# Row sums of modulation vectors begun inside the attention, two more blocks of them as row sums, and a denser pace at the long convolution

## The chip, the cores and the metric

The kernel runs on one core of one Trainium2 chip. The metric is the device time of one launch in microseconds (us). A core has a matrix engine (TensorE, PE in the rows), a vector engine (VectorE, DVE), an activation engine (ScalarE, ACT), a general engine (GpSimd, POOL) and a queue engine (SyncE, SP). They run side by side, each through its own list of instructions in a fixed order, and wait for one another by semaphores. [...]

## What is computed

A batch of one with 256 tokens of width 1024 goes through two blocks of two layers. Every layer has a mixer and a feed-forward part (FFN), and each of the two is fed by a normalised input that is scaled and shifted, and added back through a gate. The six vectors for that (two shifts, two scales, two gates, 1024 numbers each) come from a conditioning vector by one product for each layer. Of the four mixers the first is a state-space part beside an attention, the second a convolution with 31 taps, the third a latent attention, the fourth a long convolution. In short:

```python
mod = silu(c) @ mod_w[layer] + mod_b[layer]            # 1024 -> 6 * 1024, for each layer
sh1, sc1, g1, sh2, sc2, g2 = split(mod, 6)
h = rms_norm(x, norm_g) * (1 + sc1) + sh1
x = x + g1 * mixer(h)
h = rms_norm(x, norm_g) * (1 + sc2) + sh2
x = x + g2 * ffn(h)

def latent_attention(h):                               # third mixer, 16 heads
    q = rms_norm(h @ w_dq, g_q) @ w_uq                 # and a rotation of 32 of its 96 columns
    k, v = keys and values from h @ w_dkv and a context
    return softmax(q @ k.T / sqrt(96)) @ v @ w_o

def long_convolution(u):                               # fourth mixer
    x1, x2, v = split(dwconv3(u @ w_in + b_in), 3)
    v = v * x2
    return ((fftconv(v, filters) + v * d_bias) * x1) @ w_out + b_out
```

## The kernel before

**Weights.** All is float32, carried as a high and a low part. A weight comes from memory in pieces of 128 x 1024 (512 KB) on SP's queue (L434). ScalarE copies a piece into its high part `hi` (L418), VectorE makes the low part `lo` as the difference (L419), and TensorE does three products for each step of the inner dimension: high by high (L443), high by low (L445), low by high (L444). The buffers for `hi` and `lo` are three deep, so VectorE and ScalarE run at most three pieces ahead of TensorE. `linear` walks over the blocks of 128 outputs of a product, `linear_tok` does it with tokens as the rows.

**Modulation vectors.** The `mod` of a layer is 48 blocks of 128 numbers. There are two ways to get them. `modulation` gives the work to TensorE: a step loads two tiles of 512 KB on SP's queue and does two products with each (L543, `mo<-raw,cs`, 32 x 512, four records a tile); four such steps make two groups of 512 numbers, and one transposition and one sum at the end finish all. `dotted_with` gives it to VectorE as row sums, called dots here: GpSimd issues the load of one block's 128 rows (L515, `mraw<-modt`, three buffers), VectorE multiplies it by the conditioning row `crow` and sums along the row (L517, with a short read of the accumulator), and after the last block of a call adds the bias (L519).

**Their order.** `also` puts dots into a list, `later` puts steps of `modulation` into another, each with the number of the place that needs them. `tick` is called after each block of `linear` or `linear_tok` with the share of a full piece that it did: it counts, and lets one dot go for each `pace` that has been counted (and one step of `modulation` for each `every`). `need(n)` lets all go that are due by place n. `down` runs the last product of a part: it sets a pace of its own for the first blocks and 1000 for the rest. The first blocks of a product behind a normalisation (a `Front`) don't tick. A dot that the code places is then moved further by the scheduler that puts each engine's instructions in order; what it chose is fixed in the program.

**The attention.** `layer_mla` does 16 heads as eight pairs j. `scores` makes four tiles of 128 x 512 for a pair: TensorE makes `s`, VectorE its maximum (`smax`, L1533), ScalarE the exponential into `sp` with its sum (L1535), VectorE the reciprocal (`sinv`, L1536), GpSimd scales the tile by it (L1537). `turned` has TensorE transpose the four tiles (into `sx` and `ax`, L1549), ScalarE and VectorE copy them to `pt` (L1553 on VectorE), and `heads` multiplies by the values into `o` (L1565), whose low part VectorE splits off as `hl` (L419). Pairs j and j+1 overlap; the pieces of queries and keys of pair j+2 stand between, and they run out at j = 6. Behind the loop comes `w_o` by `down`. Its results go into x (L754), and the squares of x (L710, `n`) into the next norm's sum. Behind the fifth block the Front of the FFN needs the gain `a21` (L741) and makes its operands `zh` and `zl` (L304).

**Stages in time** (us from the span's start): first mixer to 187, its FFN to 333, convolution of 31 taps to about 500, its FFN with the context of the attention to about 740, latent attention to 868, `w_o` to 887, its FFN to 1078, long convolution to 1237 (its `hy_out` from 1211), last FFN to the end.

## Time and profile before

| what | before |
| --- | --- |
| time, median of 3 runs | 1439.99 us (1439.74 to 1444.86) |
| profiled execution | 1446.99 us, its span 1445.0 us |
| busy share of the span | TensorE 94%, VectorE 82%, ScalarE 58%, GpSimd 10% |
| mean granted clock of TensorE | 0.973 |
| dots | 120, of 1226 ns each |
| chain that ended last | TensorE 68%, issue 15%, VectorE 10%, ScalarE 3%, DMA 3% |

The chain that ended last is followed back from the last instruction, from each to what released it. The average says that TensorE is nearly always busy; a stage can differ from it, so the stages around the change are read one by one.

### The profile page before, as it was taken

The page shows a single profiled execution, that of the slowest core. Times are in us where ns is not written, and L with a number is a line of the kernel's source. Part 1 is how long each engine was busy: PE and PEld are TensorE (multiplying, and loading weights), DVE is VectorE, ACT ScalarE, POOL GpSimd, SP SyncE. Part 2 cuts the span into 40 slices and gives each one's busy share as a digit, 9 for nine tenths or more (in the row PEclk, how much of TensorE's full clock was granted, in tenths as well). Part 3 has the DMA queues.
Part 4 walks back from the last instruction along what each step waited for, and adds up shares of the span by engine and source line. Part 5 has one row for each costly group of instructions (what it writes and reads, how often), then busy time and mean ns, then how long its engine had stood idle before and what let it go on. Part 6 is the DMA issues. An engine that isn't in the chain of part 4 may idle for free.

```text
span 1445.0 us, 28181 instructions
## 1 busy us (share of the span) xinstructions
PE 1361.3 (94%) x10702; PEld 1238.6 (86%) x10702; DVE 1184.4 (82%) x2379; ACT 837.5 (58%) x1562; POOL 151.1 (10%) x204
## 2 busy tenths in 40 slices
PE   6988899999998899999989999999999899999997
PEld 3666799999995898999977779999999668999997
DVE  7967888878697697888769867999888978799954
ACT  5533676554474575665457645866556645776642
POOL 1053000101000000001004650000110000000000
PEclk9998999999998999999989999999999899999998
DMA  9567576888757558878635435577795556557660
GB/s 367 205 158 277 202 262 220 277 256 289 245 175 291 177 175 338 277 233 266 213 95 161 137 119 198 155 244 247 264 325 195 170 182 240 176 177 235 193 185 29
DMA packets 91988, 311.88 MB, mean 216 GB/s; under 512 B 10949, under 2 KB 13662, under 8 KB 91726
## 3 DMA queue, kind: packets, MB, share of 16 engines
q1 hardware_dynamic: 72830, 244.67, 50.7%
q0 software_dynamic: 17856, 64.36, 13.9%
q8 instruction: 84, 1.38, 0.4%
q10 hardware_dynamic: 1168, 1.06, 0.3%
q14 instruction: 50, 0.41, 0.1%
HBM read 308.73 MB, written 1.32 MB: 215 GB/s over the span
## 4 chain that ended last, share of the span: by engine, by line
PE 68%; issue 15%; DVE 10%; ACT 3%; DMA 3%; POOL 1%; DVEq 0%; SPq 0%; POOLq 0%; ACTq 0%
PE mm L443 18%; PE mm L445 18%; PE mm L444 18%; DVE lo L419 3%; PE mo L543 2%; ACT hi L418 1%; PE o L1565 1%; PE ax L1665 1%; DVE mraw L517 1%; DMA raw<-ab_in 1%; PE sx L638 1%; PE s L443 1%; PE s L444 1%; POOL mraw L515 1%; PE s L445 1%
## 5 line engine op out<-in xcount | busy, mean ns | idle before, releaser
L418 ACT ACTIVATE hi<-raw 128x1024 fp32r<-128x1024 f32 (+3 forms) x402 | 404.0, 1007 | 371.4 <-PE mm L444 285.4
L419 DVE TENSOR_TENSOR lo<-raw,hi 128x1024 fp32r<-128x1024 f32 (+3 forms) x402 | 464.1, 1161 | 121.3 <-ACT hi L418 119.5
L443 PE MATMUL mm<-hh,hi 128*128 128x256 f32 x1440 | 410.3, 288 | 14.0 <-ACT hi L418 6.4
L445 PE MATMUL mm<-hh,lo 128*128 128x256 f32 x1440 | 407.9, 285 | 5.7 <-DVE lo L419 5.7
L444 PE MATMUL mm<-hl,hi 128*128 128x256 f32 x1440 | 408.3, 285 | 1.6 <-DVE hl L1184 1.0
L443 PEld LDWEIGHTS mm<-hh,hi 128*128 128x128 f32 x1440 | 274.1, 192 | 34.7 <-issue 9.9
L445 PEld LDWEIGHTS mm<-hh,lo 128*128 128x128 f32 x1440 | 275.6, 192 | 8.4 <-DVE lo L419 6.7
L444 PEld LDWEIGHTS mm<-hl,hi 128*128 128x128 f32 x1440 | 275.5, 191 | 7.6 <-issue 3.6
L443 PE MATMUL mm<-ah,hi 128*128 128x256 f32 x704 | 199.1, 283 | 1.8 <-ACT hi L418 1.8
L445 PE MATMUL mm<-ah,lo 128*128 128x256 f32 x704 | 198.0, 282 | 2.2 <-DVE lo L419 2.0
L444 PE MATMUL mm<-al,hi 128*128 128x256 f32 x704 | 197.1, 281 | 0.0
L443 PE MATMUL mm<-zh,hi 128*128 128x258 f32 x608 | 173.7, 289 | 8.1 <-ACT zh L303 4.7
L515 POOL DMA_DIRECT2D mraw<-modt x120 | 64.1, 534 | 1096.1 <-DVE mraw L517 949.1
L445 PE MATMUL mm<-zh,lo 128*128 128x258 f32 x608 | 174.6, 288 | 0.9 <-DVE lo L419 0.7
L444 PE MATMUL mm<-zl,hi 128*128 128x258 f32 x608 | 174.0, 287 | 0.0
L517 DVE SCALAR_TENSOR_TENSOR mraw<-mraw,crow 128x1024 f32<-128x1024 f32 x120 | 145.9, 1226 | 5.7 <-DMA mraw<-modt 5.5
L445 PEld LDWEIGHTS mm<-ah,lo 128*128 128x128 f32 x704 | 132.5, 189 | 3.9 <-DVE lo L419 3.6
L443 PEld LDWEIGHTS mm<-ah,hi 128*128 128x128 f32 x704 | 132.8, 189 | 3.2 <-ACT hi L418 2.0
L444 PEld LDWEIGHTS mm<-al,hi 128*128 128x128 f32 x704 | 132.7, 189 | 1.0 <-issue 1.0
L443 PEld LDWEIGHTS mm<-zh,hi 128*128 128x128 f32 x608 | 117.1, 194 | 9.0 <-ACT zh L303 4.9
L445 PEld LDWEIGHTS mm<-zh,lo 128*128 128x128 f32 x608 | 117.2, 193 | 1.8 <-DVE lo L419 1.7
L444 PEld LDWEIGHTS mm<-zl,hi 128*128 128x128 f32 x608 | 117.9, 194 | 0.2 <-DVE zl L304 0.2
(427 smaller groups left out, 2119.8 us busy)
## 6 DMA issues: line engine op xcount, KB each, us to landing
raw<-up SPq DMA_DIRECT2D x132, 512.0 KB, 4.4
mraw<-modt POOLq DMA_DIRECT2D x120, 512.0 KB, 5.2
raw<-down SPq DMA_DIRECT2D x64, 512.0 KB, 4.4
raw<-mod SPq DMA_DIRECT2D x60, 512.0 KB, 5.2
raw<-gate SPq DMA_DIRECT2D x44, 512.0 KB, 4.7
raw<-down SPq DMA_DIRECT2D x32, 384.0 KB, 3.3
raw<-hy_in SPq DMA_DIRECT2D x24, 512.0 KB, 4.3
raw<-cm_in SPq DMA_DIRECT2D x16, 512.0 KB, 3.6
```

Source lines behind the costliest of these rows:

```text
L418: nc.scalar.activation(hi, src, AF.Copy)
L419: return nc.vector.tensor_tensor(lo, src, hi.bitcast(F32), op=ALU.subtract)
L443: nc.tensor.matmul(out, wh, xh, start=start, stop=False)
L444: nc.tensor.matmul(out, wh, xl, start=False, stop=False)
L445: self.last = nc.tensor.matmul(out, wl, xh, start=False, stop=stop)
L515: nc.gpsimd.dma_start(w, self.d[f"modt{layer}"][u])
L517: nc.vector.scalar_tensor_tensor(w, w, 1.0, row, op0=ALU.mult, op1=ALU.mult, accum_out=out[:, u : u + 1]))
L543: nc.tensor.matmul(acc[g * 32 : g * 32 + 32, :], wt, src, start=(g not in begun), stop=last)
L638: last = self.nc.tensor.matmul(st[:, c0 + t : c0 + t + 1], q[:, t * P : (t + 1) * P], self.ones[:, 0:1], start=(i == 0), stop=(i == len(sq ...
L1565: nc.tensor.matmul(o[i * 64 : i * 64 + 64], vals[:, k, c : c + 64], pt[i][:, k, :], start=(k == 0), stop=(k == 3))
L1665: nc.tensor.matmul(ps, m[:, k, m0 : m0 + P], src[:, k, s], start=(k == 0), stop=(k == 1))
```

## The change

Four things are altered. In the attention's loop over pairs a `tick` of 2.0 is added for the last three pairs, and the pace in `w_o` goes from 1.7 to 1.2. The dots of layer 2, blocks 40 to 48, and of layer 3, blocks 0 to 16, are put into the list ahead of the attention and no longer behind it. Blocks 16 to 24 of layer 3 are put there ahead of the FFN that follows and no longer at the long convolution; blocks 24 to 32, which were two of the four groups that `modulation` did at the long convolution, become dots beside them, and the steps of `modulation` that are left come at every fourth count and no longer at every second. In the convolution with 31 taps the pace goes from 2.0 to 1.5.

```diff
@@ -1584,9 +1584,11 @@
                 else:
                     qq = qq[1:] * 2
                 heads(j, pt)
+                if j > 4:
+                    self.tick(2.0)
             self.dump("mla_o", oh.bitcast(F32))
             self.need(6.5)
-            self.down(d["w_o"], oh, ol, self.residual(x, g1, sq, front=front), 1.7, acc=both)
+            self.down(d["w_o"], oh, ol, self.residual(x, g1, sq, front=front), 1.2, acc=both)
 
 
     def hy_filters(self, fp, hp, H):
@@ -1851,7 +1853,7 @@
 
         self.later(4, self.modulation(1, range(6, 9), cs, mods[1:2]), 1000.0)
         self.later(5, self.modulation(2, range(4), ("c_2", "c_ctx_2"), (mods[2], modc)), 2.0)
-        self.pace(2.0)
+        self.pace(1.5)
         self.also(4, 1, 36, 40, row, mods[1])
         f2.norm(self.stats(sq, D))
         sq = []
@@ -1907,6 +1909,8 @@
 
             e.close()
             sq = []
+            self.also(8, 2, 40, 48, row2[0], mods[2])
+            self.also(9, 3, 0, 16, row2[0], mods[3])
             f = front(7, 2, 3, "a21", "norm_ffn_g_2", 0)
             with self.banks(mm=2, s=2, ax=1, o=1):
                 self.layer_mla(x, f2, None, six(2, 2), sq, ckh, ckl, pe, final, f)
@@ -1914,8 +1918,8 @@
         self.dump("x4", x)
         e.enter_context(self.more(4))
         self.pace(3.0)
-        self.also(8, 2, 40, 48, row2[0], mods[2])
-        self.also(9, 3, 0, 16, row2[0], mods[3])
+        self.also(10, 3, 16, 24, row2[0], mods[3])
+        self.also(11, 3, 24, 32, row2[0], mods[3])
         f.norm(self.stats(sq, D))
         sq = []
         f2 = front(9, 3, 0, "a30", "norm_mix_g_2", 8)
@@ -1926,8 +1930,7 @@
             H = hyp.tile([P, 4, D], F32, name="H")
             f2.norm(self.stats(sq, D))
             self.pace(1.5)
-            self.later(11, self.modulation(3, range(6, 10), cs, mods[3:]), 2.0)
-            self.also(10, 3, 16, 24, row2[0], mods[3])
+            self.later(11, self.modulation(3, range(8, 10), cs, mods[3:]), 4.0)
             sq = []
             f = front(11, 3, 3, "a31", "norm_ffn_g_2", 8)
             self.layer_hy(x, f2, None, six(3, 2), sq, hyp, H, f)
```

The order of the instructions shows it as follows. Names with a number are tiles; `mraw` is a dot's tile.

At the end of the attention, VectorE before, from the first score tile of the last pair:

```order
L1533 TENSOR_REDUCE smax_10560<-s_10556 128x1
L1536 RECIPROCAL sinv_10443<-ssum_10442 128x1
L419 TENSOR_TENSOR hl_9343<-o_10519,hh_9342 128x256
L1533 TENSOR_REDUCE smax_10572<-s_10568 128x1
L1553 COPY pt4_10530<-ax_10537 128x4x128
L1536 RECIPROCAL sinv_10562<-ssum_10561 128x1
L1533 TENSOR_REDUCE smax_10584<-s_10580 128x1
L1536 RECIPROCAL sinv_10574<-ssum_10573 128x1
```

And in the changed kernel:

```order
L1533 TENSOR_REDUCE smax_10567<-s_10563 128x1
L1536 RECIPROCAL sinv_10569<-ssum_10568 128x1
L419 TENSOR_TENSOR hl_9343<-o_10519,hh_9342 128x256
L517 SCALAR_TENSOR_TENSOR mraw_10530,mod2_80<-mraw_10530,crow_7941 128x1024
L1533 TENSOR_REDUCE smax_10579<-s_10575 128x1
L1553 COPY pt4_10537<-ax_10544 128x4x128
L1533 TENSOR_REDUCE smax_10591<-s_10587 128x1
L519 TENSOR_TENSOR mod2_80<-mod2_80,p1_882 128x16
L517 SCALAR_TENSOR_TENSOR mraw_10534,mod2_80<-mraw_10534,crow_7941 128x1024
L1536 RECIPROCAL sinv_10581<-ssum_10580 128x1
```

Two dots now stand here. The reciprocal of the first tile (before `sinv_10562`, now `sinv_10569`) has moved ahead of both; a dot stands ahead of the maximum of the second tile (`smax_10579`), and another ahead of its reciprocal (before `sinv_10574`, now `sinv_10581`).

GpSimd at the same place before, from the last scaling of the pair before the last:

```order
L1537 TENSOR_SCALAR sp_10445<-sp_10445,sinv_10443 128x512
L1537 TENSOR_SCALAR sp_10564<-sp_10564,sinv_10562 128x512
L1537 TENSOR_SCALAR sp_10576<-sp_10576,sinv_10574 128x512
L1537 TENSOR_SCALAR sp_10588<-sp_10588,sinv_10586 128x512
L1537 TENSOR_SCALAR sp_10600<-sp_10600,sinv_10598 128x512
L515 DMA mraw_11878<-modt2 128x1024
```

And in the changed kernel:

```order
L1537 TENSOR_SCALAR sp_10445<-sp_10445,sinv_10443 128x512
L1537 TENSOR_SCALAR sp_10571<-sp_10571,sinv_10569 128x512
L515 DMA mraw_10662<-modt2 128x1024
L515 DMA mraw_10735<-modt2 128x1024
L1537 TENSOR_SCALAR sp_10583<-sp_10583,sinv_10581 128x512
L1537 TENSOR_SCALAR sp_10595<-sp_10595,sinv_10593 128x512
L1537 TENSOR_SCALAR sp_10607<-sp_10607,sinv_10605 128x512
L515 DMA mraw_10774<-modt2 128x1024
```

Two loads of dots now stand between the first and the second scaling of the last pair.

VectorE at the start of `w_o`, before, from the last low part of the attention's output:

```order
L419 TENSOR_TENSOR hl_9343<-o_10641,hh_9342 128x256
L754 SCALAR_TENSOR_TENSOR x_88<-s_10652,mod2_80,x_88 128x256
L754 SCALAR_TENSOR_TENSOR x_88<-mm_10686,mod2_80,x_88 128x256
L754 SCALAR_TENSOR_TENSOR x_88<-s_10726,mod2_80,x_88 128x256
L419 TENSOR_TENSOR lo_10766<-raw_10763,hi_10765 128x1024
L419 TENSOR_TENSOR lo_10802<-raw_10799,hi_10801 128x1024
L419 TENSOR_TENSOR lo_10838<-raw_10835,hi_10837 128x1024
L710 TENSOR_TENSOR n_10720<-n_10684,n_10718 128x256
L517 SCALAR_TENSOR_TENSOR mraw_10722,mod2_80<-mraw_10722,crow_7941 128x1024
```

And in the changed kernel:

```order
L419 TENSOR_TENSOR hl_9343<-o_10651,hh_9342 128x256
L517 SCALAR_TENSOR_TENSOR mraw_10662,mod2_80<-mraw_10662,crow_7941 128x1024
L754 SCALAR_TENSOR_TENSOR x_88<-s_10665,mod2_80,x_88 128x256
L754 SCALAR_TENSOR_TENSOR x_88<-mm_10699,mod2_80,x_88 128x256
L754 SCALAR_TENSOR_TENSOR x_88<-s_10738,mod2_80,x_88 128x256
L419 TENSOR_TENSOR lo_10781<-raw_10778,hi_10780 128x1024
L419 TENSOR_TENSOR lo_10820<-raw_10817,hi_10819 128x1024
L419 TENSOR_TENSOR lo_10859<-raw_10856,hi_10858 128x1024
L304 SCALAR_TENSOR_TENSOR zl_10894<-x_88,a21_10891,zh_10893 128x256
L710 TENSOR_TENSOR n_10733<-n_10697,n_10731 128x256
```

A dot has come between the last `hl` and the first result of `w_o`, and ahead of the three low parts that follow. Counted by the pieces of weights that stand ahead of them, the changed kernel has eight dots in the attention's last part and `w_o` where the one before had one: four between the last key piece and the first piece of `w_o` (one behind the last `hl`), and four in `w_o`. In the FFN behind, 24 dots become 23, at the same places.

VectorE in `hy_out` of the long convolution before, from a sum of squares ahead of the gain `a31`:

```order
L710 TENSOR_TENSOR n_15093<-n_15047,n_15091 128x256
L754 SCALAR_TENSOR_TENSOR x_88<-n_15126,mod3_81,x_88 128x256
L570 TENSOR_REDUCE mod3_81<-ax_15143 128x16
L571 TENSOR_TENSOR mod3_81<-mod3_81,p1_882 128x16
L741 SCALAR_TENSOR_TENSOR a31_15226<-mod3_81,p1_882 128x8
L419 TENSOR_TENSOR lo_15288<-raw_15285,hi_15287 128x1024
L710 TENSOR_TENSOR n_15131<-n_15093,n_15129 128x256
L419 TENSOR_TENSOR zl_15229<-mod3_81,zh_15228 128x8x2
L304 SCALAR_TENSOR_TENSOR zl_15229<-x_88,a31_15226,zh_15228 128x256 x2
```

And in the changed kernel:

```order
L517 SCALAR_TENSOR_TENSOR mraw_15043,mod3_81<-mraw_15043,crow_7941 128x1024
L754 SCALAR_TENSOR_TENSOR x_88<-n_15077,mod3_81,x_88 128x256
L570 TENSOR_REDUCE mod3_81<-ax_15136 128x8
L419 TENSOR_TENSOR lo_15281<-raw_15278,hi_15280 128x1024
L571 TENSOR_TENSOR mod3_81<-mod3_81,p1_882 128x8
L710 TENSOR_TENSOR n_15082<-n_15041,n_15080 128x256
L754 SCALAR_TENSOR_TENSOR x_88<-n_15115,mod3_81,x_88 128x256
L741 SCALAR_TENSOR_TENSOR a31_15219<-mod3_81,p1_882 128x8
L419 TENSOR_TENSOR lo_15331<-raw2_15328,hi_15330 128x1024
L710 TENSOR_TENSOR n_15120<-n_15082,n_15118 128x256
L517 SCALAR_TENSOR_TENSOR mraw_15122,mod3_81<-mraw_15122,crow_7941 128x1024
L304 SCALAR_TENSOR_TENSOR zl_15222<-x_88,a31_15219,zh_15221 128x256 x4
```

Two dots have come in, one ahead of the reduction of `mod3` and one ahead of the first `zl`. On TensorE the eight steps of `modulation` in the long convolution have become four: those that ran at 1130.5, 1165.8, 1191.9 and 1219.3 us are gone. In the convolution with 31 taps there were three dots, at 435.0, 442.5 and 470.9 us; now one stands three pieces ahead of the first of these, one behind the products `cmY` of the middle columns that followed it, and one where the third was.

## Rows read from the trace of the kernel before

**Rows 1.** The page: engines; groups by line with busy us, mean ns, idle

```profile
PE 1361.3 (94%) x10702; PEld 1238.6 (86%) x10702; DVE 1184.4 (82%) x2379; ACT 837.5 (58%) x1562; POOL 151.1 (10%) x204
...
L515 POOL DMA_DIRECT2D mraw<-modt x120 | 64.1, 534 | 1096.1 <-DVE mraw L517 949.1
...
L517 DVE SCALAR_TENSOR_TENSOR mraw<-mraw,crow 128x1024 f32<-128x1024 f32 x120 | 145.9, 1226 | 5.7 <-DMA mraw<-modt 5.5
```

**Rows 2.** By stage: length; busy us of PE, PEld, DVE, ACT, POOL; clock; DMA

```profile
870.00:895.00 25.00, 24.42 (x183) 23.58 (x184) 19.79 (x37) 15.08 (x28) 0.58 (x1) 0.93 0.68 225
895.00:1080.00 185.00, 181.68 (x1514) 179.90 (x1513) 171.65 (x308) 117.03 (x201) 12.67 (x24) 1.00 0.74 242
...
1125.00:1180.00 55.00, 50.40 (x233) 30.59 (x231) 44.02 (x88) 30.94 (x53) 2.11 (x4) 0.91 0.56 182
...
1220.00:1250.00 30.00, 27.94 (x230) 26.32 (x227) 21.87 (x48) 20.24 (x40) 0.00 (x0) 1.00 0.59 211
```

**Rows 3.** Windows of 10 us at the start of `w_o`

```profile
870.00:880.00 10.00, 9.56 (x65) 9.33 (x66) 7.61 (x12) 5.28 (x9) 0.58 (x1) 0.83 0.70 235
880.00:890.00 10.00, 9.94 (x80) 9.45 (x79) 9.36 (x18) 8.16 (x16) 0.00 (x0) 1.00 0.67 243
```

**Rows 4.** Timeline of GpSimd, last scalings: start, us, instruction, idle before

```profile
852.45 6.19 POOL L1537 TENSOR_SCALAR sp<-sp,sinv 128x512 f32<-128x512 f32 x4 [1.74 <-DVE sinv L1536]
```

**Rows 5.** Timeline of VectorE, last score tiles

```profile
850.07 0.42 DVE L419 TENSOR_TENSOR hl<-o,hh 128x256 fp32r<-128x256 f32 x1 [1.22 <-ACT hh L418]
...
852.57 0.69 DVE L1533 TENSOR_REDUCE smax<-s 128x1 f32<-128x512 f32 x1 [0.28 <-PE s L445]
853.18 0.15 DVE L1536 RECIPROCAL sinv<-ssum 128x1 f32<-128x1 f32 x1
```

**Rows 6.** Timeline of TensorE, last transpositions and heads

```profile
864.06 0.66 PE L1549 MATMUL ax<-ident,sp 128*128 128x128 f32 x4
865.60 1.91 PE L1565 MATMUL o<-pt,vals 128*64 128x256 f32 x14 [0.88 <-DVE pt L1553]
```

**Rows 7.** Timeline of VectorE at the start of `w_o`

```profile
868.99 0.48 DVE L754 SCALAR_TENSOR_TENSOR x<-s,mod,x 128x256 f32<-128x256 f32 x1 [0.61 <-PE s L445]
...
873.91 1.22 DVE L517 SCALAR_TENSOR_TENSOR mraw<-mraw,crow 128x1024 f32<-128x1024 f32 x1
```

**Rows 8.** Timeline of TensorE, first blocks behind `w_o`

```profile
890.20 0.39 PE L445 MATMUL mm<-zh,lo 128*128 128x258 f32 x1
```

**Rows 9.** Timeline of GpSimd, two earlier scalings

```profile
778.91 2.63 POOL L1537 TENSOR_SCALAR sp<-sp,sinv 128x512 f32<-128x512 f32 x1 [5.10 <-DVE sinv L1536]
...
820.90 1.56 POOL L1537 TENSOR_SCALAR sp<-sp,sinv 128x512 f32<-128x512 f32 x1 [3.10 <-DVE sinv L1536]
```

**Rows 10.** Timeline of VectorE, the dots beside those scalings

```profile
778.97 1.22 DVE L517 SCALAR_TENSOR_TENSOR mraw<-mraw,crow 128x1024 f32<-128x1024 f32 x1
...
821.90 1.22 DVE L517 SCALAR_TENSOR_TENSOR mraw<-mraw,crow 128x1024 f32<-128x1024 f32 x1
```

**Rows 11.** Tile `mo`, long convolution: count, ns, first and last start

```profile
L543 PE MATMUL mo<-raw,cs x64: 592/604/618, 1130.5 to 1224.5; 128*32 128x512 f32 x64
```

**Rows 12.** Timeline of TensorE at the long convolution

```profile
1144.11 2.73 PE L1649 MATMUL ax<-l_hy_w,fb 64*128 64x512 f32 x4 [2.46 <-DVE dt L1652]
...
1165.79 1.07 PE L543 MATMUL mo<-raw,cs 128*32 128x512 f32 x8
...
1219.29 1.06 PE L543 MATMUL mo<-raw,cs 128*32 128x512 f32 x8
1220.29 0.39 PE L443 MATMUL mm<-hh,hi 128*128 128x256 f32 x1
```

**Rows 13.** Timeline of VectorE at the long convolution

```profile
1178.94 1.28 DVE L1721 TENSOR_TENSOR Y<-H,mm 128x512 f32<-128x512 f32 x2 [3.98 <-PE ax L1665]
...
1225.17 1.23 DVE L419 TENSOR_TENSOR lo<-raw,hi 128x1024 fp32r<-128x1024 f32 x1 [1.10 <-ACT hi L418]
```

**Rows 14.** Timeline of VectorE at the convolution with 31 taps

```profile
444.37 0.42 DVE L1347 TENSOR_TENSOR dt<-cmH,mm 128x256 f32<-128x256 f32 x1 [0.38 <-PE mm L1343]
```

## The prediction, made before the changed kernel had run

> **What bounds the kernel now.** I read the page first, then windows by stage, then timelines at the places that the change touches. The page says that TensorE is busy 94% of the time and VectorE 82% [rows 1]. A dot costs VectorE 1.226 us and 0.08 us for the reading of its sum, 1.31 us in all, and GpSimd 0.53 us for the issue of its load [rows 1]. Whether a dot costs time at all depends on the stage. In the FFN behind the attention TensorE does 181.68 us of work in 185 us, and VectorE 171.65 us: both are nearly full, TensorE is the bound [rows 2]. At the start of `w_o`, from 870 to 895 us, VectorE has 19.79 us of work in 25 us, and between 880 and 890 us 9.36 of 10 [rows 2, 3]; the first block behind it waits at 890.20 us for a low part that VectorE has only just made [rows 8]. That is the seam where more dots can be felt. At the long convolution TensorE is busy 50.40 of 55 us, but at the lower of its clocks for part of it (granted clock 0.91), and it waits there for VectorE, 2.46 us in one piece at 1144.11 [rows 2, 12]. What is taken from TensorE there is won only where VectorE does not end last.
>
> **The change, part by part.** The sum is made against the profiled execution, 1446.99 us with a span of 1445.0; the median of the runs, 1439.99, lies 7.0 lower, and I carry the difference over unchanged.
>
> *A, the last pair of the attention.* Four more row sums lie between the last key piece and `w_o`, where there was none. VectorE has room: three of the four lie beside the last scores, and the fourth is counted in B. The path to watch is the one through GpSimd, which is in order. Before, it does the last four scalings in one run, from 852.45 to 858.64 us, 1.55 us each [rows 4]. Now two loads stand behind the first of them, and each can be issued only when a dot has freed its buffer. I walk VectorE through its new order: the low part `hl` at 850.07 as before [rows 5], the first dot to 851.8, the maximum of the second tile to 852.4, a copy to 853.0, the maximum of the third (852.57 before [rows 5]) to 853.6, the second dot to 855.0. Then comes the reciprocal of the second tile, at 853.18 before [rows 5]. GpSimd's second load is issued at 855.0 to 855.5, and three scalings follow: the last ends at 860.2 and not at 858.64, 1.6 us late. But TensorE wants the last tile only at 864.06, since products of `w_o` stand ahead of it in its own order, and the heads follow at 865.60 [rows 6]. The cover is 3.8 us, so A costs 0. Were it gone, it would cost two dots and two issues, 2 x 1.31 + 2 x 0.53 = 3.7; from below, the gain `a21` and its shift leave the seam, some 0.3 us. Bounds: -0.3 to +3.7.
>
> A row bears on this: a scaling at 778.91 that began together with a dot took 2.63 us and not 1.56, 1.07 longer [rows 9, 10]. Another, at 820.90, still took 1.56 with a dot begun at 821.90 beside it, and that dot was not held either [rows 9, 10]. If each of the three dots stretched a scaling by 1.07, the last would end 3.2 us later still and the cover would shrink from 3.8 to 0.6 us: the sum stays, the chance of the slow rival grows, and I give that rival 0.08 rather than 0.05.
>
> [...]
>
> *B, `w_o` and the first blocks behind it.* By the order a dot stands between the last `hl` and the first result of `w_o`, and four dots follow where one stood (873.91 [rows 7]): four more, 4 x 1.31 = 5.24 us of VectorE. Queued behind them are the updates of x, three low parts, and with them TensorE. The loads are no matter, they were issued in the attention. VectorE has 2.39 + 0.64 = 3.03 us free between 870 and 890 us [rows 3], and 0.61 us ahead of 868.99 [rows 7]. What is left over, 5.24 - 3.03 - 0.61 = 1.6 us, meets a TensorE that has no lead at 890.20 [rows 8]. B costs +1.6; bounds 0 (the splits `zl` now spread forward into the holes) and +5.2 (no hole is hit).
>
> *C, the FFN behind.* The order shows that 24 dots become 23: dots begun earlier make room, and the blocks 16 to 32 of layer 3 fill it. All of TensorE's idle time there is 185 - 181.68 = 3.3 us [rows 2], or 0.14 for each dot. C is -0.1; bounds -1.3 (a whole dot) and 0.
>
> *D, TensorE at the long convolution.* Four of eight steps go, eight records each. One takes 1.06 us, with 1.00 to the next product [rows 12]; the 64 records of `mo`, at a median of 604 ns each, overlap four at a time, which gives the same eight steps from 1130.5 to 1224.5 [rows 11]. The step at 1130.5 lies ahead of TensorE's wait for VectorE at 1144.11 [rows 12]: nothing won. The one at 1165.79 lies ahead of VectorE's wait of 3.98 us for TensorE at 1178.94 [rows 12, 13]: 1.0 won. The one at 1191.9, among the 64 records [rows 11], I count like the first, since this stretch too has VectorE making what TensorE waits for: nothing. The one at 1219.29 is followed at once by the next product of `hy_out` [rows 12], where TensorE is the bound (27.94 of 30 us [rows 2]): 1.0 won. D is -2.0; bounds -4.0 and 0. The eight loads of the removed steps leave SP's queue and eight come to GpSimd's; the bytes are the same, and none of the waits in the rows ends on one of them.
>
> *E, two dots in `hy_out`.* They cost 2.62 us of VectorE, which has 30 - 21.87 = 8.1 us free in this stage [rows 2]. The first meets a gap of 1.10 us at 1225.17 [rows 13], 0.2 us too short; the second, ahead of the first `zl`, I put at the same. E is +0.4; bounds 0 and +2.6.
>
> *F, the convolution with 31 taps.* The dot at 442.5 goes from a place where the next product waits for TensorE by 0.38 us anyway [rows 14], to one ahead of it. F is 0; bounds one dot each way, -1.3 and +1.3.
>
> The sum: 0 + 1.6 - 0.1 - 2.0 + 0.4 + 0 = -0.1 us, so 1446.9 for the profiled execution and **1439.9 us** for the median. All ends together would be -6.7 and +11.8.
>
> **The rivals.** *Faster:* the holes of VectorE at the seam take the dots (B 0), all four steps of TensorE are won (D -4.0), the one dot fewer in the FFN is won whole (C -1.3), and `hy_out` hides its two (E 0): -5.3, 1434.7 us. For it speaks that VectorE's idle time is larger than the added dots in each stage but `w_o`; against it the wait at 1144.11.
>
> *Nothing won at the long convolution:* the exchange of TensorE's work for VectorE's takes place where VectorE ends last. D is 0, E 2.6, B and C as forecast: 1.6 - 0.1 + 2.6 = +4.1, 1444.1 us. For it speaks TensorE's wait at 1144.11 [rows 12], against it the 3.98 us in which VectorE waits for TensorE [rows 13].
>
> *Slower:* VectorE becomes the bound at the seam. All seven added dots between the last keys and the FFN are then felt, 7 x 1.31 = 9.2 us, with the other terms as forecast (-0.1 - 2.0 + 0.4 = -1.7): +7.5, 1447.5 us. It decides when the last scaling ends later than 864 us, and the dot ahead of `w_o`'s first result finds TensorE waiting. The low clock that stands there already, 0.83 from 870 to 880 us [rows 3], would last longer then. Against it speaks the cover of 3.8 us.
>
> **How the numbers follow.** The forecast, a gain and a loss that cancel, has a chance of 0.60; the faster case 0.20; nothing won at the long convolution 0.12; the seam as the bound 0.08. The forecast's own range is 1437 to 1442. To leave out no more than 2 in 10, the range takes in the faster case and the third, and leaves the slow one out: 1434 to 1444.5. A measurement of this kernel can tell 0.5%, 7.2 us, from no change. Faster than 1432.8 would take more than all terms at their best; for what the shuffled order may add I give it 0.05. Slower than 1447.2 is the slow rival and what else piles up: 0.07. The rest, 0.88, is within.
>
> **What would show it.** In the trace of the changed kernel: the last four scalings with a gap behind the first and an end near 860 us (A); the heads at 865 to 866 us after the stage's start is aligned; the first block behind `w_o` waiting for a low part by 1 to 2 us more (B); the FFN as long as before within 1 us (C); VectorE's wait near 1179 us shorter by 1 us (D); `hy_out` shorter by 0.5 to 1 us (D and E). The prediction is wrong if the scheduler's new order on TensorE, in stages that the change does not name, moves the time by more than its terms, or if the first kept dot at the seam is late because its load is.

## The result: slower, by 0.65%

The changed kernel takes 1453.11 us (median of 4 runs, 1452.66 to 1454.09), the kernel before 1442.42 us in the runs beside it: a ratio of 1.0065, with a 95% interval from 1.0039 to 1.0091. Timed again with 12 runs, the ratio was 1.0064 (1.0043 to 1.0085). The forecast was 1439.9 us, no change, with a range from 1434 to 1444.5. It was wrong at the start of `w_o`, where the largest part of the loss is (step B), and in the size of step F; a further part of the loss lies where no term stood.

(In the title, "long convolution" is a slip for the convolution with 31 taps, whose pace is the one that was changed. Below, "long convolution" is the mixer of the fourth layer, as in the text ahead.)

Runs of one and the same program differ here by some 3 us each way and at times by more, and with them the profiled ones. The median of the twelve later runs of the changed kernel is 1449.99 us, 3.1 under that of the first four. The first profile of the kernel before, 1446.99 us, lay 4.6 us above the median of its timed runs (1442.42); a second one, taken later, took 1439.72 us. So stages are compared over several profiles. TensorE starts 8976 products of weights (lines 443 to 445) in each kernel, so the time from the start of one of them to the start of another measures the same work, as long as the products stand in the same order around the two. The table gives it for seven stretches, bounded by the products numbered 2000, 2700; 4500, 4860, 5160; 6500, 7360, 7700, 8970. Only 4860 is not quite the same place in each: by then the changed kernel has done the three products of one more score tile and three fewer of `w_o`, some 0.35 us of work.

| us, by stretch | before, two profiles | changed, two profiles | difference of the means |
| --- | --- | --- | --- |
| convolution with 31 taps (2000 to 2700) | 128.40, 126.44 | 128.89, 130.11 | +2.1 |
| attention (4500 to 4860) | 111.75, 111.90 | 113.22, 113.16 | +1.4 |
| `w_o` and first blocks behind it (4860 to 5160) | 52.10, 50.96 | 57.79, 55.22 | +5.0 |
| FFN behind the attention (5160 to 6500) | 163.78, 164.08 | 162.86, 164.04 | -0.5 |
| long convolution (6500 to 7360) | 165.74, 164.78 | 163.59, 163.32 | -1.8 |
| end of `hy_out`, last FFN's start (7360 to 7700) | 46.08, 46.06 | 47.48, 48.85 | +2.1 |
| last FFN (7700 to 8970) | 153.48, 151.86 | 156.04, 154.44 | +2.6 |

The seven sum up to 10.9 us. That this is near the difference of the first medians, 10.7, is partly luck: the two pairs of profiled executions differ by 6.9 us, and the stretches left out (0 to 2000 and 2700 to 4500) took the changed kernel 4.0 us less. Over all profiles of this study these two vary from 338.7 to 345.2 and from 236.4 to 243.3 us.

The page of the changed kernel shows none of this; it has hardly moved, but for eight dots (its rows answer to [rows 1]):

```profile
PE 1358.9 (94%) x10670; PEld 1240.4 (85%) x10670; DVE 1193.6 (82%) x2396; ACT 837.5 (58%) x1562; POOL 153.8 (11%) x212
...
L517 DVE SCALAR_TENSOR_TENSOR mraw<-mraw,crow 128x1024 f32<-128x1024 f32 x128 | 155.9, 1228 | 3.1 <-DMA mraw<-modt 3.0
```

**The seam.** TensorE's timeline behind `w_o` in the changed kernel (start, duration, instruction, idle before and its releaser) has the last product of `w_o` and the first of the FFN. Where the kernel before went on at once and waited a little later for a low part [rows 8], there are now 3.04 us of nothing:

```profile
888.16 0.28 PE L445 MATMUL mm<-hh,lo 128*128 128x256 f32 x1
891.48 0.55 PE L443 MATMUL mm<-zh,hi 128*128 128x258 f32 x1 [3.04 <-DVE x L754]
```

What it waits for is an update of x on VectorE, whose timeline beside it is this:

```profile
888.24 0.42 DVE L710 TENSOR_TENSOR n<-n 128x256 f32<-128x256 f32 x1
888.57 1.23 DVE L517 SCALAR_TENSOR_TENSOR mraw<-mraw,crow 128x1024 f32<-128x1024 f32 x1
889.71 0.09 DVE L517 DVE_READ_ACCUMULATOR mraw<-mraw,crow 128x1 f32 x1
889.71 1.23 DVE L419 TENSOR_TENSOR lo<-raw,hi 128x1024 fp32r<-128x1024 f32 x1
890.85 0.49 DVE L754 SCALAR_TENSOR_TENSOR x<-mm,mod,x 128x256 f32<-128x256 f32 x1
```

TensorE finished the last block of `w_o` at about 888.4 us (888.16 + 0.28). VectorE could have added it to x then, but had the sum of squares, a dot (888.57), its read, and a low part (889.71) ahead of it in its list, and came to it at 890.85. Why the next block needs that update is not in the profile but in the program: the accumulator of the FFN's first block lies in the PSUM bank in which that of `w_o`'s last block lay, and the bank is free only when VectorE has read it. In the kernel before, the FFN's first block lay in the bank of the sixth block of `w_o`, read at 883.36, and started at 886.59, ahead of the last update at 888.53 (its VectorE, then its TensorE):

```profile
883.36 0.48 DVE L754 SCALAR_TENSOR_TENSOR x<-mm,mod,x 128x256 f32<-128x256 f32 x1
...
888.53 0.48 DVE L754 SCALAR_TENSOR_TENSOR x<-mm,mod,x 128x256 f32<-128x256 f32 x1
```

```profile
886.59 0.28 PE L443 MATMUL mm<-zh,hi 128*128 128x258 f32 x1
```

The windows of 10 us that answer to [rows 3], of the changed kernel (length, then busy us of TensorE, its weight loads, VectorE, ScalarE and GpSimd with counts, then the granted clock of TensorE as a share of full speed; the last two are the DMA's share and GB/s), show VectorE full or nearly so from 870 to 890, and a lower clock behind the wait in this profile, 0.66 from 890 to 900:

```profile
870.00:880.00 10.00, 8.56 (x55) 7.94 (x55) 10.00 (x19) 6.13 (x10) 1.05 (x2) 0.83 0.80 230
880.00:890.00 10.00, 8.44 (x72) 8.23 (x71) 9.57 (x16) 7.99 (x13) 1.05 (x2) 1.00 0.98 374
890.00:900.00 10.00, 8.52 (x49) 8.55 (x50) 5.04 (x13) 2.17 (x5) 0.53 (x1) 0.66 0.55 194
```

In the second profile of the changed kernel the same wait, 3.02 us, is followed by a granted clock of 1.00 over the next 10 us, and the stretch takes 55.22 us for 57.79.

**The attention's tail** went as forecast on the path through GpSimd. GpSimd's timeline (it answers to [rows 4]) has the two loads behind the first scaling, and the last scaling ends at 856.44 + 4.64 = 861.08 us:

```profile
852.85 0.58 POOL L515 DMA_DIRECT2D mraw<-modt  x1 [0.51 <-DVE mraw L517]
855.87 0.53 POOL L515 DMA_DIRECT2D mraw<-modt  x1 [2.45 <-DVE sinv L1536]
856.44 4.64 POOL L1537 TENSOR_SCALAR sp<-sp,sinv 128x512 f32<-128x512 f32 x3
```

TensorE reaches the last transposition at 865.21 and the heads at 866.74, 1.1 us later than in [rows 6], but it waits there for the copy `pt` by about the same time as before (0.87 and 0.88 us), and not for a scaling:

```profile
865.21 0.66 PE L1549 MATMUL ax<-ident,sp 128*128 128x128 f32 x4
866.74 1.91 PE L1565 MATMUL o<-pt,vals 128*64 128x256 f32 x14 [0.87 <-DVE pt L1553]
```

Another path was touched. Some 11 us earlier TensorE waits 0.74 us for the copy of an earlier tile, a wait that the kernel before does not have. That copy stands on VectorE behind the tail's first dot, which ran from 851.14 to 852.54 us, and a maximum:

```profile
853.08 0.68 DVE L1553 COPY pt<-ax 128x512 f32<-128x512 f32 x1
```

```profile
853.90 0.63 PE L1549 MATMUL ax<-ident,sp 128*128 128x128 f32 x4 [0.74 <-DVE pt L1553]
```

**The last FFN's first block**, behind `hy_out`, has two waits that the kernel before does not have there:

```profile
1242.20 0.74 PE L443 MATMUL mm<-zh,hi 128*128 128x258 f32 x2 [1.84 <-ACT zh L418]
1243.65 0.39 PE L444 MATMUL mm<-zl,hi 128*128 128x258 f32 x1 [0.71 <-DVE zl L419]
```

The kernel before has two others a little further on, the longer of them this one, which the changed kernel does not have:

```profile
1248.58 0.68 PE L657 MATMUL sx<-ident,ny 128*128 128x128 f32 x4 [1.69 <-DVE ny L651]
```

### The profile page after: what moved, and what is told of

Its sections match the earlier page's. It is cut to its first block, busy times and chain, and to the rows that moved or that the text cites. A ratio compares the mean times of both kernels' runs of the same rounds, so it can differ in the third digit from the quotient of the medians.

```text
span 1452.3 us, 28130 instructions
## 1 busy us (share of the span) xinstructions
PE 1358.9 (94%) x10670; PEld 1240.4 (85%) x10670; DVE 1193.6 (82%) x2396; ACT 837.5 (58%) x1562; POOL 153.8 (11%) x212
## 4 chain that ended last, share of the span: by engine, by line
PE 69%; issue 14%; DVE 10%; ACT 3%; DMA 3%; POOL 1%; DVEq 0%; POOLq 0%; SPq 0%; ACTq 0%
PE mm L443 19%; PE mm L445 18%; PE mm L444 18%; DVE lo L419 2%; PE mo L543 2%; PE ax L1667 1%; ACT hi L418 1%; DMA mraw<-modt 1%; DMA raw<-ab_in 1%; PE o L1565 1%; DVE mraw L517 1%; POOL mraw L515 1%; PE sx L638 1%; DVE e L769 1%; PE s L443 1%
## 5 line engine op out<-in xcount | busy, mean ns | idle before, releaser
L419 DVE TENSOR_TENSOR lo<-raw,hi 128x1024 fp32r<-128x1024 f32 (+3 forms) x402 | 464.4, 1161 | 132.9 <-ACT hi L418 130.1
L515 POOL DMA_DIRECT2D mraw<-modt x128 | 68.4, 534 | 1096.4 <-DVE mraw L517 951.6
L517 DVE SCALAR_TENSOR_TENSOR mraw<-mraw,crow 128x1024 f32<-128x1024 f32 x128 | 155.9, 1228 | 3.1 <-DMA mraw<-modt 3.0
```

Of the source, the lines that this page charges most:

```text
L419: return nc.vector.tensor_tensor(lo, src, hi.bitcast(F32), op=ALU.subtract)
L515: nc.gpsimd.dma_start(w, self.d[f"modt{layer}"][u])
L517: nc.vector.scalar_tensor_tensor(w, w, 1.0, row, op0=ALU.mult, op1=ALU.mult, accum_out=out[:, u : u + 1]))
```

## The experiments

Two theories stood at the start. **Bank**: the loss at the seam is the wait for the bank, set by the update of x behind a dot and a low part. **Load**: the four extra dots in `w_o` make VectorE late, whatever the bank.

**1. The pace at the convolution back to 2.0.** This one number, 400 us ahead of the seam, turns out to decide the bank: the accumulators `mm` take turns on two banks, and in the built program the turn at `w_o` is the other one with 1.5 (why, was not followed up). With 2.0 the FFN's first block is in the bank of `w_o`'s sixth block again.

```diff
-        self.pace(1.5)
+        self.pace(2.0)
         self.also(4, 1, 36, 40, row, mods[1])
```

> The changed kernel with the pace at the convolution of 31 taps put back from 1.5 to 2.0. Nothing is moved at the end of the attention or in w_o by this, and every dot there stays; but the first block of the FFN behind w_o now sits in the PSUM bank of w_o's sixth block and no longer in that of its last. Theory 1 (bank: TensorE waits for the update of x that frees the bank, and a dot and a low part stand ahead of that update on VectorE): the wait of 3.0 us at 891.48 goes, and with it most of the slow clock behind it; 4 to 5 us less than the changed kernel, about 1448.5 us. Theory 2 (load: the four extra dots in w_o make VectorE late, whatever the bank): no change there, 1452 to 1453.5 us.

Measured: 1447.69 us (7 runs, 1438.94 to 1455.84), ratio 1.0035 (1.0002 to 1.0068), 5.4 us less than the first four runs of the changed kernel and 2.3 less than the twelve later ones. TensorE's timeline has no wait at the FFN's first block (887.62), and small ones for low parts behind it:

```profile
887.51 0.28 PE L445 MATMUL mm<-hh,lo 128*128 128x256 f32 x1
887.62 0.28 PE L443 MATMUL mm<-zh,hi 128*128 128x258 f32 x1
...
890.25 0.39 PE L445 MATMUL mm<-zh,lo 128*128 128x258 f32 x1 [0.30 <-DVE lo L419]
891.04 0.39 PE L444 MATMUL mm<-zl,hi 128*128 128x258 f32 x1 [0.40 <-DVE zl L304]
```

VectorE's has the sixth and the last update of x:

```profile
885.18 0.48 DVE L754 SCALAR_TENSOR_TENSOR x<-mm,mod,x 128x256 f32<-128x256 f32 x1
...
890.11 0.48 DVE L754 SCALAR_TENSOR_TENSOR x<-mm,mod,x 128x256 f32<-128x256 f32 x1
```

The last update still comes late, at 890.11, with its dot ahead of it, as in the changed kernel; nobody waits for it. Theory bank is confirmed as to the wait. But the stretch from 4860 to 5160 still takes 54.25 us, 2.7 more than the mean of the two profiles before (51.5): the load has a part of its own.

**2. Another bank by the turn of the accumulators.**

```diff
             self.need(6.5)
+            next(turn)
             self.down(d["w_o"], oh, ol, self.residual(x, g1, sq, front=front), 1.2, acc=both)
```

> The changed kernel with the two rings of accumulators, which w_o's blocks take in turn, taken in the other order in w_o (one step of the turn ahead of it). The dots stay, the pace at the convolution stays at 1.5; the first block of the FFN now sits in the bank of w_o's seventh block, whose update stands one dot and one low part earlier than that of the last. Theory 1 (bank): the wait of 3.0 us becomes under 0.7 us; 3 to 5 us less than the changed kernel, 1448 to 1450 us. Theory 2 (load): 1452 to 1453.5 us.

Measured: 1446.07 us (8 runs), ratio 1.0042 (1.0020 to 1.0064), 7.0 us less than the first runs of the changed kernel and 3.9 less than the later ones. Instead of one wait of 3.3 us from start to start there are two, of 0.63 and 1.07; the second was not expected. This edit also moves products of `w_o` ahead of heads of the attention, so that the product numbered 4860 is another place in runs 2, 7 and 8, and their stretches on both sides of it can't be set beside the others'. Two different edits that move the bank and leave the dots take the wait away and give back 2 to 7 us by the medians, by the ratios about 0.2 to 0.3%, with intervals that overlap the changed kernel's; what the two share is the bank.

**3. No dots in `w_o`.** The pace of `w_o` at 1000 in place of 1.2.

> The changed kernel without dots in w_o (its pace 1000 in place of 1.2; four dots go on to the FFN behind); the bank of the last block is still the one that the FFN's first block waits for. Theory 1 (bank): the update that frees it loses the dot ahead of it, the wait becomes 1 to 2 us; 2 to 4 us less, 1449 to 1451 us. Theory 2 (load): all of the loss at the seam goes, 5 to 6 us, 1447 to 1448 us, with at most 1 us given back in the FFN, which has no room for four more.

Measured: 1453.00 us (4 runs), nothing won. At the seam the theory's number came: the wait fell from 3.3 to 1.6 us from start to start. But the four dots were not taken by the FFN. They were let go by `need` at the end of `hy_out`, where the last FFN's first block waits for them:

```profile
1248.84 0.80 PE L443 MATMUL mm<-zh,hi 128*128 128x258 f32 x2 [13.08 <-ACT zh L418]
```

So the run tells nothing by its time, and much about the place where leftover dots end.

**4. The pace at the convolution alone, on the kernel before.** The same line as in the first run, 2.0 to 1.5, and nothing else.

> The kernel before with only the pace at the convolution of 31 taps changed from 2.0 to 1.5. By the order of VectorE nothing changes at the attention and in w_o, but the first block of the FFN sits in the bank of w_o's last block. Theory 1 (bank): TensorE waits at the FFN's first block from 886.6 to about 889, since the update of x stands at 888.53: +2 to +3 us over the kernel before. Theory 2 (load): nothing, within 1 us of the kernel before; the convolution itself within 1 us by either.

Measured: 1446.27 us (8 runs), ratio 1.0032 (1.0013 to 1.0050). TensorE, and the updates of x on VectorE:

```profile
884.38 0.28 PE L445 MATMUL mm<-hh,lo 128*128 128x256 f32 x1
887.54 0.36 PE L443 MATMUL mm<-zh,hi 128*128 128x258 f32 x1 [2.88 <-DVE x L754]
```

```profile
884.20 0.48 DVE L754 SCALAR_TENSOR_TENSOR x<-s,mod,x 128x256 f32<-128x256 f32 x1
884.60 1.67 DVE L304 SCALAR_TENSOR_TENSOR zl<-x,a,zh 128x256 fp32r<-128x256 f32 x4
886.18 0.42 DVE L710 TENSOR_TENSOR n<-n 128x256 f32<-128x256 f32 x1
886.51 0.48 DVE L304 SCALAR_TENSOR_TENSOR zl<-x,a,zh 128x256 fp32r<-128x256 f32 x1
886.91 0.48 DVE L754 SCALAR_TENSOR_TENSOR x<-mm,mod,x 128x256 f32<-128x256 f32 x1
```

With no dot more at the seam TensorE waits 2.88 us for the last update. It stands behind four `zl`, a sum of squares and another `zl`. Theory load could not give this; the bank alone costs 3 us.

**5. The changed kernel again**: 1449.99 us (12 runs), the ratio given above, 2 us under what was expected, and 3.02 us of wait at the same place in a second profile.

> The changed kernel as it is, timed again beside the others. Theories 1 (bank) and 2 (load) say the same: 10 us over the kernel before, 1452 to 1454 us, with TensorE's wait of about 3 us at the FFN's first block behind w_o.

**6. The parts at the attention alone, on the kernel before**: the ticks, the pace 1.2 in `w_o`, and the two lists ahead of the attention. The bank is that of the sixth block.

> The kernel before with the parts at the attention alone: the ticks in the last three pairs, the pace 1.2 in w_o, and the dots of layer 2, 40 to 48, and of layer 3, 0 to 16, in the list ahead of the attention. The exchange at the long convolution and the pace at the convolution of 31 taps stay as before, and the FFN's first block then sits in the bank of w_o's sixth block. Theory 1 (bank): the four dots in the attention's tail and the four in w_o cost 1 to 2.5 us there in all, no wait for the update of x; the same time as the kernel before within 3 us, 1441 to 1446 us, the FFN being relieved by eight dots. Theory 2 (load): 4 to 5 us lost between 880 and 900 us, 1446 to 1449 us.

Measured: 1449.02 us (12 runs), ratio 1.0049 (1.0033 to 1.0065). Here theory bank failed, and load gave the right number: without the bank's wait the dots cost 6.4 us, of which the stretch from 4860 to 5160 (54.63 us) shows 3.1. The FFN was relieved by seven dots (17 for 24) and was no shorter (163.87 us against 163.78 and 164.08). TensorE's waits behind `w_o` are now for low parts of weights and of x:

```profile
891.36 0.38 PE L445 MATMUL mm<-zh,lo 128*128 128x258 f32 x1 [0.50 <-DVE lo L419]
892.14 0.39 PE L444 MATMUL mm<-zl,hi 128*128 128x258 f32 x1 [0.41 <-DVE zl L304]
...
894.01 0.38 PE L444 MATMUL mm<-zl,hi 128*128 128x258 f32 x1 [0.53 <-DVE zl L304]
```

**7. The convolution's pace with another bank, on the kernel before**: the edits of runs 4 and 2 together.

> The kernel before with the pace at the convolution of 31 taps at 1.5, as in the fourth run, and with the two rings of accumulators in w_o taken in the other order: the FFN's first block sits in the bank of w_o's seventh block. Theory 1 (bank): of the 4.4 us that the fourth run lost between 882 and 914 us, 2.5 to 4 go; within 2 us of the kernel before there. If the pace itself, or the clock, had made that loss, it would stay at 4.4 us.

Measured: 1443.29 us (12 runs), ratio 1.0002 (0.9983 to 1.0021). Run 4's loss is gone, so it was the bank's.

**8. The changed kernel with the other bank and a denser pace at the long convolution.** As run 2, and:

```diff
             f2.norm(self.stats(sq, D))
-            self.pace(1.5)
+            self.pace(1.2)
             self.later(11, self.modulation(3, range(8, 10), cs, mods[3:]), 4.0)
```

> The changed kernel with the other bank (as in the second run) and with the pace at the long convolution 1.2 in place of 1.5, so that the two dots of blocks 24 to 32 that stood in hy_out are done before it. If the gain of the removed steps of TensorE was partly lost to the wait for the shift of the next norm (2.1 and 1.1 us at the last FFN's first block, 0 and 0.65 before), 2 to 3 us come back there: 1442 to 1445 us, about the kernel before or a little under. If VectorE is the bound at the long convolution, the two dots only move the loss ahead: as the second run, 1446 us.

Measured: 1443.58 us (12 runs), ratio 1.0010 (0.9993 to 1.0027), 2.5 us under run 2. The stretch from 7360 to 7700 takes 46.18 us (49.18 in run 2, 46.07 before). Run 2 shows what the wait was. VectorE has the second dot, four `zl`, an update of x, and only then the addition of the bias (L519) that completes the shift of the next norm:

```profile
1232.29 1.22 DVE L517 SCALAR_TENSOR_TENSOR mraw<-mraw,crow 128x1024 f32<-128x1024 f32 x1
...
1233.44 1.67 DVE L304 SCALAR_TENSOR_TENSOR zl<-x,a,zh 128x256 fp32r<-128x256 f32 x4
1235.02 0.48 DVE L754 SCALAR_TENSOR_TENSOR x<-n,mod,x 128x256 f32<-128x256 f32 x1
1235.42 0.16 DVE L519 TENSOR_TENSOR mod<-mod,p 128x8 f32<-128x8 f32 x1
```

TensorE's first block needs that shift in its two extra columns. ScalarE makes the high part of it, and comes to it 1.4 us behind the addition, since it stands in ScalarE's list behind the high part of a piece of weights, which had waited for TensorE, and two more instructions. In run 8 no dot is in `hy_out`, and this wait is gone:

```profile
1237.02 0.20 ACT L418 ACTIVATE zh<-mod 128x16 fp32r<-128x16 f32 x1
```

```profile
1237.27 0.74 PE L443 MATMUL mm<-zh,hi 128*128 128x258 f32 x2 [1.84 <-ACT zh L418]
```

**9 and 10. Run 6 without its dots in `w_o`, and without its ticks.** Pace 1000 in `w_o` in the one; the two lines of the tick left out in the other.

> The sixth run (the parts at the attention alone, the FFN's first block in the bank of w_o's sixth block) without dots in w_o: only the four of the attention's tail are left of the seam. That run lost 6.4 us in the timed runs. If the dots in w_o make it (VectorE has 3.0 us free there for 5.2 us of dots), 2 to 4 us come back, 1445 to 1447 us. If the dots in the tail make it (GpSimd's loads between the scalings, the last scaling at 861 us), it stays at 1448.5 to 1450 us.

> The sixth run without the ticks in the last three pairs: no dot in the attention's tail, four dots in w_o as before them, and the loads of the dots in GpSimd's list behind the scalings. If the tail makes the loss of 6.4 us, 2 to 4 us come back, 1445 to 1447 us, and the scalings end at 858.6 as in the kernel before. If the dots in w_o make it, it stays at 1448.5 to 1450 us or gets worse by 1 us, since two dots stand in a row behind the three low parts.

Measured: run 9 1443.95 us (12 runs), ratio 1.0007 (0.9986 to 1.0028); run 10 1447.50 us (12 runs), ratio 1.0027 (1.0006 to 1.0049). Run 9 is better than either expectation. With the four dots of the tail alone the loss is gone, and the longest wait of the first blocks is 0.25 us:

```profile
892.81 0.39 PE L443 MATMUL mm<-zh,hi 128*128 128x258 f32 x1 [0.25 <-ACT zh L303]
```

Run 10 lies between its two expectations, and its interval reaches into both. With the dots in `w_o` alone the stretch from 4860 to 5160 is as long as in run 6 (55.05 and 54.63 us), and by yet another last link. Three of the dots stand ahead of the gain `a21`. It comes 32.6 us behind the product numbered 4860 (879.28 - 846.64), against 30.5 in the first profile of the kernel before (882.07 - 851.55). The fourth dot stands between the gain and the first `zl` that is made with it, which comes 37.3 us behind that product (883.98 - 846.64) for 33.9 before (885.42 - 851.55). TensorE stands 3.58 us for one of these `zl`:

```profile
879.28 0.16 DVE L741 SCALAR_TENSOR_TENSOR a<-mod,p 128x8 f32<-128x8 f32 x1
...
883.98 1.27 DVE L304 SCALAR_TENSOR_TENSOR zl<-x,a,zh 128x256 fp32r<-128x256 f32 x3
```

```profile
884.52 0.58 PE L444 MATMUL mm<-zl,hi 128*128 128x258 f32 x1 [3.58 <-DVE zl L304]
```

**11. The kernel before, profiled once more.**

> The kernel before, profiled once more. The first profile of it took 1446.99 us, 4.4 us over the median of its timed runs (1442.6). If that excess lies in stages that the change does not touch (ahead of the attention), the stage by stage comparison from the attention on stands as it is; if it lies between 840 and 905 us, the seam of the changed kernel has lost more than the comparison of the first two profiles shows, by up to 4 us.

Measured: 1439.72 us. Its last product of weights starts 6.9 us earlier than in the first profile; of these, 2.0 lie in the convolution with 31 taps, 1.4 in the FFN ahead of the attention, 1.1 between 4860 and 5160, and 1.6 in the last FFN. Beside this second profile the seam of the changed kernel has lost about 1 us more than beside the first.

**12. What was left standing, put together.** Run 1 and no dots in `w_o`; in place of them denser paces:

```diff
-        self.pace(3.0)
+        self.pace(2.4)
         self.also(10, 3, 16, 24, row2[0], mods[3])
...
-            self.pace(1.5)
+            self.pace(1.0)
             self.later(11, self.modulation(3, range(8, 10), cs, mods[3:]), 4.0)
```

> What the runs so far left standing, together: the four dots in the attention's tail stay, none in w_o (pace 1000), the pace at the convolution of 31 taps 2.0, which also puts the FFN's first block into the bank of w_o's sixth block; the exchange of two blocks stays, with the dots that it needs at a denser pace in the FFN (2.4 for 3.0) and at the long convolution (1.0 for 1.5), so that none is left for hy_out. From the ninth run (0.8 us over the kernel before) and 1 to 1.5 us won by four steps of TensorE fewer: 0 to 1 us under the kernel before, 1441.5 to 1443.5 us. If dots in the FFN, where TensorE is the bound, or at the long convolution cost more than a quarter of their length each (seven more dots, 9.2 us of VectorE), 2 to 3 us over it.

Measured: 1443.15 us (12 runs), ratio 1.0000 (0.9979 to 1.0021). The long convolution takes 162.72 us, 2.5 less than before, and the FFN 165.55, 1.6 more. By this interval the change can be had at no loss, and it wins nothing: no kernel of this study beats the one before.

## Why the prediction was wrong, step by step

Of the 13.2 us between the forecast and the first measurement, 2.4 are the base: a fourth run moved the median of the kernel before from 1439.99 to 1442.42 us. The rest is gone through by the terms. The ends of the terms add up to -6.9 and +12.8, not to -6.7 and +11.8 as the prediction has it; nothing in it hangs on that.

**A, the attention's tail (0): held in the sum,** but not because nothing waited. The last scaling ended at 861.1 us, forecast 860.2; TensorE did not wait for it. It did wait for a copy that a dot had made late (853.90 above). From the product numbered 4500 to that numbered 4911, the first behind the last heads and with the same work ahead of it in these runs, the two profiles before take 128.2 and 128.3 us and run 10, without dots in the tail, 128.3; runs 1, 6, 9 and 12, with the four dots, take 129.1 to 129.3. So the four dots bring TensorE 1.0 us late to the end of the attention. Where no dots stand in `w_o` it is made up there: run 9 takes 33.9 us from 4911 to 5160, for 35.7 and 34.5 before, and costs 0.8 us in all, which can't be told from nothing. The changed kernel itself takes 130.15 and 130.09 us up to 4911. The further 0.9 us lies between the products 4600 and 4650, where its granted clock is 0.86 and 0.88, and 1.00 in the twelve other profiles; run 3, with the same bank and the same four dots, has 1.00. Why the clock fell there stays open.

**B, `w_o` (+1.6, bounds 0 to +5.2): this step failed.** The stretch lost 5.0 us by the two pairs of profiles (4.5 if it is begun at 4911), and runs 6 and 9, which differ in the pace of `w_o` alone, lie 5.1 us apart in time, of which the stretch shows 3.3 (54.63 and 51.36 us). Two things were wrong in its working. First, the sum set the dots against VectorE's free time between 870 and 890 us, as if holes anywhere in it could be used. But VectorE works through a list, and each of the four dots stood ahead of something that TensorE was about to need: a low part, a `zl`, the gain, or the update of x. Which of these ended last differed from run to run of the study (runs 1, 6 and 10), the price hardly did: 2.7 to 3.5 us in that stretch over the mean of before. Second, the bank was not in the working at all. In the kernel before, the next block could start at 886.59 us, before the last update of x at 888.53, only because its bank had been read at 883.36. The edit of the pace at the convolution moved the bank, and the wait became 3 us (runs 4 and 7 apart by 3.0 us in time). The two prices don't add up fully (run 6 +6.4, run 4 +3.5, the changed kernel +7.4 beside run 6). It would fit that a late update and late low parts hide behind each other, but this was not tried apart.

**C, the FFN (-0.1): held,** with -0.5. Runs 6 and 12 show that little relief could be had there: seven dots fewer made it no shorter, while two more and another spacing made it 1.6 us longer.

**D, TensorE at the long convolution (-2.0): held in size,** with -1.8; the place was right in part. The 0.91 that the prediction gives for the granted clock from 1125 to 1180 us is a mean: by windows of 1 us the profile before has 0.50 from 1144 to 1154 and 1.00 in nearly all the rest. Between the products 6900 and 7100, where the removed steps of 1130.5 and 1165.8 us stood, 1.7 us is won, forecast 1.0; VectorE's wait near 1179 fell from 3.98 to 2.26 us. Around the step of 1219.3 (7250 to 7300) 0.2 is won, forecast 1.0.

**E, two dots in `hy_out` (+0.4, bounds 0 to +2.6): held in the changed kernel, and by luck.** I had sized the second dot by a gap on VectorE, and not asked who waits for the result of it. It completes the shift that the next layer's first block takes in. In run 2 this costs 3.2 us against run 8 (25.1 and 21.9 us from the product 7360 to 7500). In the changed kernel the wait is there too, but the one of 1.69 us that the kernel before has behind it is not: 21.5 and 22.9 us, for 22.1 and 22.0 before, 0.2 more on the mean. The +2.1 of the table lies elsewhere, in its last twenty products (7680 to 7700), which take 4.2 and 4.3 us for 2.4. There TensorE waits at 1282.96 and 1283.73 us (0.99 and 0.38) for the normalised operand. Run 9 has these two waits and no dot in `hy_out`, run 2 has both dots and not these waits, so they are not the dots'. No term stood for them, and their cause stays open.

**F, the convolution (0, bounds -1.3 to +1.3): mis-sized.** Over all profiles the stretch from 2000 to 2700 takes 125.8 to 128.4 us at the pace of 2.0 (7 kernels' profiles, mean 127.3) and 128.3 to 130.1 at 1.5 (7, mean 129.0), 1.7 us more. In most profiles TensorE's granted clock is lower behind the moved dot, by the windows from the product numbered 2490 to that numbered 2500, of the changed kernel and of the second profile of the kernel before:

```profile
437.01:466.90 29.89, 22.12 (x136) 13.61 (x135) 19.13 (x71) 12.57 (x33) 1.58 (x3) 0.83 0.77 289
```

```profile
436.86:463.66 26.80, 19.39 (x134) 12.54 (x133) 20.09 (x75) 12.58 (x32) 1.59 (x3) 0.91 0.84 304
```

By all fourteen profiles it is 0.78 to 0.83 with the denser pace, and 0.88 to 0.94 with the old one but for the first profile of the kernel before, which has 0.77. Runs 4 and 7 have this edit without the others and take 128.3 and 128.8 us there, so it goes with the pace and not with the dots of the attention; whether and how the dot behind the products `cmY` lowers the clock was not tried apart.

**The last FFN (nothing forecast)** lost 2.6 us between the pairs of profiles. About 1.5 of it is the clock over the forty products from 7760 to 7800, which is granted at 0.73 in both profiles of the changed kernel and at 0.74 in run 1, and at 1.00 in the other eleven; why stays open. Another 1.2 us need not be the change's: over the 900 products from 8000 to 8900, at a granted clock of 1.00 throughout, they follow each other by 120.0 and 118.7 ns in the changed kernel's two profiles and by 118.7 and 117.3 in the two before, so executions of one kernel differ by as much.

**The rivals.** The slow one was the right one in its place, VectorE as the bound at the seam, and nearest in its size: 1447.5 us, measured 1453.1 and 1450.0. Its condition, a last scaling later than 864 us, did not come true (861.1), so the nearness is partly luck. Nor did the low clock there last longer: from 870 to 880 us it is 0.83 in the first profile of the changed kernel, as in that of the kernel before. It was given 0.08, on the ground that VectorE had enough idle time in sum, and on the cover of 3.8 us in the tail, which was real but guarded another place.

## What to carry to other kernels

Work that is put on an engine with idle time must be priced by what stands right behind it in that engine's list, and by who waits for that, not by the idle time of the stage. Where a block's accumulator changes hands, ask which reader must have emptied the bank: a shift by one in the turn of the banks, caused far away, can put the last update of one product ahead of the first of the next. When dots or like fillers are taken out of one place, look where the last call that lets all go will put them.

## What the runs showed of the hardware

A dot of VectorE and a scaling of GpSimd that overlap can take longer than alone. Which of them does, and by how much, went with their starts in these profiles, and it repeats to about a hundredth of a microsecond. Over all fourteen profiles, where a scaling alone takes about 1.55 us and a dot 1.22:

| the dot starts, against the scaling | scaling, us | dot, us | seen in |
| --- | --- | --- | --- |
| 0.62 us before | 2.03 | 1.21 | runs 2, 8 |
| 0.19 before | 2.46 | 1.22 | runs 1, 6, 9, 12 |
| 0.06 to 0.07 behind | 2.63 to 2.64 | 1.22 | all fourteen profiles |
| 0.15 behind | 1.57 | 1.61 to 1.62 | runs 2, 8 |
| 0.36 behind | 1.57 to 1.58 | 1.40 to 1.41 | the changed kernel (twice), run 3 |
| 0.9 to 1.5 behind | 1.55 to 1.57 | 1.21 to 1.22 | nine profiles |

For the second row these are the lines of run 9, and for the fifth the dot of the changed kernel, beside the third of three scalings:

```profile
855.83 2.46 POOL L1537 TENSOR_SCALAR sp<-sp,sinv 128x512 f32<-128x512 f32 x1 [0.58 <-DVE mod L519]
```

```profile
855.63 1.22 DVE L517 SCALAR_TENSOR_TENSOR mraw<-mraw,crow 128x1024 f32<-128x1024 f32 x1
```

```profile
851.14 1.40 DVE L517 SCALAR_TENSOR_TENSOR mraw<-mraw,crow 128x1024 f32<-128x1024 f32 x1
```

In the first three rows the scaling ends 1.35 to 1.44 us behind the end of the dot, 0.11 to 0.20 less than the 1.55 it takes alone. In the next two the dot ends 1.76 us behind the start of the scaling, both times: less its own 1.22, that is 0.54 us behind this start, about a third of the scaling. In the last row the dot starts later than that, and both take as long as alone. Why the lengths go this way, no run shows.

The pair at 778.91 us [rows 9, 10] is of the third row: the scaling's recorded start is the earlier one by 0.06 us, and yet it is the scaling that took longer, 2.63 us.
